# One-hot matmuls of the experts on whole fp32 values in place of split fp32r halves

## Chip, core and metric

One Trainium2 chip, of which the program uses one core. A core has a matrix engine (PE), which loads a stationary operand (PEld) and streams a moving one past it into PSUM banks of 512 fp32 columns, and the engines DVE, ACT and POOL, which work on SBUF and (DVE, ACT) read PSUM; SP issues most DMAs. The metric is the device time of one execution in microseconds.

## What is computed

Two layers. Each has token mixing, cross-attention into 256 memory tokens and a mixture of 32 experts in four groups, all over 512 tokens of 1024 features:

```python
def hierarchical_moe(x, w_group, b_group, w_router, b_router, w_gate, w_up, w_down):
    g_p, g_idx = lax.top_k(g_prob, 1)              # top-1 group
    ...
    e_p, e_idx = lax.top_k(jax.nn.softmax(e_sel, axis=-1), 2)   # top-2 experts in it
    weights = g_p * (e_p / jnp.sum(e_p, -1, keepdims=True))
    ...
    for e in range(N_EXPERTS):
        h = jax.nn.silu(t @ w_gate[e]) * (t @ w_up[e])
        out = out + (h @ w_down[e]) * gate[:, e:e + 1]
```

followed by `layer_norm(ALPHA * x + moe)`. All inputs and outputs are fp32.

## The kernel before

**Routing.** `proj_residual` makes the cross-attention's output by tiles of 128 tokens and calls `router_tile` (L1161 on) for each of the four. It normalises the tile, transposes it on PE, multiplies it with the router's weights (L1178), picks two experts on DVE, and counts with small one-hot products (L1207 to L1209) which slot each token takes; every expert has 64 slots. The two slot numbers of a token give a one-hot matrix `oh` of 128 tokens by 256 slots (L1219, L1220).

**Split values.** PE takes fp32 operands in two ways here. A tile typed fp32r is a reduced form of a value, and one product is one instruction. Where the full value is wanted, `split` (L355) makes a high part on ACT (L356) and the rest on DVE (L357), and each product is made from the parts. A tile typed fp32 goes to PE as it is, and the trace then shows two MATMUL instructions (and two weight loads) for each product that the program writes: the two products of L786, with 128 by 512 outputs, stand in it as four in each layer.

**First gather.** `router_tile` splits the tokens of its tile into `X[0]` and `X[1]`, two pages of 16 KB per partition from the pool of the tag `T16`, which has four. `gather_first` collects the slots of experts 0 to 3: for each token tile and each of eight feature blocks two products, one with each part (L1340), into four banks of 256 slots by two blocks.

**Experts.** `moe` runs 16 pairs of experts. A pair's 12 weight pages of 512 KB come from `moe_raw`, a ring of 30 pages; 12 of them lie in three `T16` pages, so that ring and tokens share that pool. For pair p, PE has two runs, whose order `run_of` fixes. In the first stand the down projection of pair p-1 (`down`, L1395, 8 products on whole fp32 weights) and the up projection of pair p (`up`, L1372, 16 products); the two experts of a pair take one half of the array each, side by side. In the second stand the transposes of the rows fetched for pair p+1 (`fetched`, L1325), the products that give token numbers in every other pair up to 11 (L1304), the transposes of the activations (`turn`, L1385) and the scatter of pair p-1.

**Scatter.** `down` leaves the pair's output in PSUM. ACT scales it into `y[0]`, typed fp32r (L1397), and DVE makes the rest `y[1]` (L1398). `scatter` (L1513 on) adds the rows back to their tokens: for each of four token tiles and two halves of the features two products of the one-hot `ohT` with `y[0]` and `y[1]` into a bank of the tag `sm` (L1518), and DVE adds the bank to `x` (L1522; L1524 with sums after the last pair). That tag has four banks, which the transposes use too. Tokens over 64 per expert go through `overflow`, a loop over blocks of 64 that ends with the same scatter (L1597 to L1604).

Of the kernel before, what the change touches and what calls it, by code (L numbers as in the profile page):

```python
# [9 lines left out]
F32R = mybir.dt.float32r  # L10
F16 = mybir.dt.float16
I32 = mybir.dt.int32
U32 = mybir.dt.uint32
AF = mybir.ActivationFunctionType
OP = mybir.AluOpType
# [6 lines left out]
P = 128  # L22
T = 512
NT = 4
D = 1024
# [185 lines left out]
class K:  # L211
# [932 lines left out]

    def router_state(self, l):
        r = {"rw": self.router_weights(l), "lg": self.bank(), "rk": self.bank()}
        X = [self.t([P, NT, D], "T16", 4, F32R, self.tp) for _ in range(2)]
        r["X"] = [[z[:, t, :] for t in range(NT)] for z in X]
        for n in ("gm", "em"):
            r[n] = self.t([P, NT, 8], "r" + n)  # L1150
        r["oh"] = [self.t([P, NT, NE], f"roh{i}") for i in range(2)]
        r["M"] = self.t([P, NT, NE], "rM", dt=F16)
        r["ge"], r["V"] = (self.t([P, NT, NE], n) for n in ("rge", "rV"))
        r["s"] = self.t([P, NT, 2], "rs")
        r["oh0"] = self.t([P, NT, 256], "oh", 2, F32R, self.mp)
        return r

    def router_tile(self, x, t, st, r):


        nc = self.nc  # L1161
        tt, ts = nc.vector.tensor_tensor, nc.vector.tensor_scalar
# [33 lines left out]
        oh = [o[:, t, :] for o in r["oh"]]  # L1196
        for i in range(2):
            ts(oh[i], io[:, 0:NE], ef[:, i:i + 1], None, op0=OP.is_equal)
        chosen = tt(M[:, t, :], oh[0], oh[1], op=OP.add)
        if t == NT - 1:  # L1200
            with self.tc.issue_after(chosen.ins):
                self.split(r["X"][0][t], r["X"][1][t], x)
        else:
            self.split(r["X"][0][t], r["X"][1][t], x)
        o = r["rk"][:, t * NE:(t + 1) * NE]
        for u in range(t):
            nc.tensor.matmul(o, self.ones16, M[:, u, :], start=u == 0, stop=False)  # L1207
# [118 lines left out]
        for k in range(4):  # L1326
            self.gathered(l, Xs, 4 * g + k, ps[:, k * n:(k + 1) * n])

    def gather_first(self, l, Xs, oh, X):

        nc, v = self.nc, self.vec[l]
        banks = [self.bank(self.pj if i < 3 else None) for i in range(4)]
        for ps in banks:
            nc.tensor.matmul(ps, self.zero16, self.zero16[:, 0:1].to_broadcast([P, 512]), start=True, stop=False)

        def add(t):
            for f in range(KC):
                ps = banks[f // 2][:, (f % 2) * 256:(f % 2 + 1) * 256]
                for i in range(2):
                    nc.tensor.matmul(ps, X[i][t][:, f * P:(f + 1) * P], oh[:, t, :], start=False,  # L1340
                                     stop=f % 2 == 1 and i + t == NT)
                if t == NT - 1 and f % 2:
                    for j in range(2):
                        self.gathered(l, Xs, f - 1 + j, banks[f // 2][:, j * 256:(j + 1) * 256])
        return add
# [7 lines left out]
    def experts(self, Xs, gu, dn, ws, page, dpage=None):  # L1353
# [34 lines left out]

        def down(hf, run):
            if hf == 0:  # L1390
                y.extend(self.t([P, D], "e_y", 2, F32R, self.mp) for _ in range(2))
            po, c = self.bank(self.pj), slice(hf * 512, (hf + 1) * 512)
            for k in range(2):
                for i in range(n):
                    run.append(nc.tensor.matmul(po[CAP * i:CAP * i + CAP, :], st["hT"][:, k, CAP * i:CAP * i + CAP],  # L1395
                                                st["w"][k][i][:, c], start=k == 0, stop=k == 1))
            nc.scalar.activation(y[0][0:R, c], po[0:R, :], AF.Copy, scale=ws)  # L1397
            nc.vector.scalar_tensor_tensor(y[1][0:R, c], po[0:R, :], ws, y[0][0:R, c], op0=OP.mult, op1=OP.subtract)  # L1398

        y = []  # L1400
        return up, act, turn, down, y
# [16 lines left out]

        self.fill = self.memory(l, range(self.n_gap), self.load_memT(page), page, lambda: self.t([P, T], "e_s", 4, pool=self.mp))

    def moe(self, l, r, X, x, following):

        nc, a = self.nc, self.a
        s = r["s"]
# [2 lines left out]
        place = lambda n: (first[:, :, 128 * n:128 * n + 128] if n < 2 else  # L1427
                           XX[:, n % 3].rearrange("p (k s) -> p k s", k=KC))
        oh16 = XX[:, 3].bitcast(F16).rearrange("p (i t s) -> p i t s", i=2, t=NT)
        add = self.gather_first(l, first, r["oh0"], X)  # L1430
        for t in range(NT):
            add(t)
        ix = self.slot_tokens(s, 1, oh16[:, 0])([])
# [58 lines left out]
    def onehot_rows(self, srow, p, ws):  # L1492

        nc = self.nc
        ohT, junk = self.t([P, T], "e_oT", 2, F32R, self.mp), self.t([P, T], "e_j", 1, F16, self.mp)
        pi, w2 = self.c("pidx")[:, p:p + 1], self.t([P, 2], "ew2", 2)
        for i in range(2):
            nc.vector.scalar_tensor_tensor(junk, srow[i], pi, srow[2 + i], op0=OP.is_equal, op1=OP.mult, accum_out=w2[:, i:i + 1])
        nc.vector.tensor_tensor(ws[:, p:p + 1], w2[:, 0:1], w2[:, 1:2], op=OP.add)
        nc.vector.tensor_scalar(ohT, srow[0], pi, None, op0=OP.is_equal)  # L1500
        nc.vector.scalar_tensor_tensor(ohT, srow[1], pi, ohT, op0=OP.is_equal, op1=OP.add)
        return ohT
# [10 lines left out]
    def scatter(self, x, y, ohT, t, hf, total=None, run=None):  # L1513

        nc = self.nc
        ps, c, n = self.bank(), slice(hf * 512, (hf + 1) * 512), ohT.shape[0]
        for i in range(2):
            m = nc.tensor.matmul(ps, ohT[:, t * P:(t + 1) * P], y[i][0:n, c], start=i == 0, stop=i == 1)  # L1518
            if run is not None:
                run.append(m)  # L1520
        if total is None:
            nc.vector.tensor_tensor(x[t][:, c], x[t][:, c], ps, op=OP.add)  # L1522
        else:
            nc.vector.scalar_tensor_tensor(x[t][:, c], ps, 1.0, x[t][:, c], op0=OP.mult, op1=OP.add, accum_out=total)  # L1524

    def overflow_block(self, l, r):
# [2 lines left out]
        nc = self.nc  # L1529
        so = r["s2"]  # L1530
        Xs, ws = self.t([P, KC, CAP], "T16", 4, pool=self.tp), self.t([P, 1], "mow")
        ohT = self.t([P, T], "e_oT", 2, F32R, self.mp)
        o2 = self.t([P, 2, NT, 2, CAP], "e_y", 2, pool=self.mp)
        oh = self.t([P, NT, 2, CAP], "e_y", 2, pool=self.mp)
        io = self.c("iota")[:, 0:CAP].unsqueeze(1).to_broadcast([P, 2, CAP])
# [25 lines left out]
    def overflow(self, l, r, x, sums):  # L1561
# [3 lines left out]
        with self.tc.For_i(0, n, 1) as i:  # L1565
# [26 lines left out]
            for k in range(2):  # L1592
                for hf in range(2):
                    nc.tensor.matmul(po[CAP * hf:CAP * hf + CAP, :], hT[:, k, :], d[k][:, hf * 512:(hf + 1) * 512],
                                     start=k == 0, stop=k == 1)
            y = [self.t([P, D], "e_y", 2, F32R, self.mp)[:, 0:512] for _ in range(2)]
            nc.scalar.activation(y[0], po, AF.Copy, scale=ws)  # L1597
            nc.vector.scalar_tensor_tensor(y[1], po, ws, y[0], op0=OP.mult, op1=OP.subtract)
            for t in range(NT):
                for hf in range(2):  # L1600
                    ps, c, rows = self.bank(), slice(hf * 512, (hf + 1) * 512), slice(CAP * hf, CAP * hf + CAP)
                    for v in y:
                        nc.tensor.matmul(ps, ohT[rows, t * P:(t + 1) * P], v[rows], start=v is y[0], stop=v is y[1])
                    nc.vector.scalar_tensor_tensor(x[t][:, c], ps, 1.0, x[t][:, c], op0=OP.mult, op1=OP.add,  # L1604
                                                   accum_out=sums[:, t, hf:hf + 1])

# [54 lines left out]
    def layer(self, l, x_src, xT):  # L1661
# [34 lines left out]
        e2, self.e2 = self.open("e2")  # L1696
        self.n_raw = 0
        r = self.router_state(l)
        X = r["X"]
        self.proj_residual(l, PI_XO, oT, x, None, lambda t, st, gb: self.router_tile(x[t], t, st, r),  # L1700
                           lambda: self.t([P, 1024], "e1", self.n_e1, F32R, self.e1))
        last = l == L - 1
        x = self.moe(l, r, X, x, None if last else l + 1)
        if not last:
            xT = self.new_xT()
            self.filler("x3")
# [45 lines left out]
```

## Time and profile before

| | us |
|---|---|
| median of 3 runs | 1554.85 |
| lowest and highest | 1550.07, 1559.25 |
| the profiled execution | 1561.04 |
| its span in the trace | 1559.2 |
| PE busy in it | 1478.3 |
| DVE busy in it | 1054.6 |
| experts' pairs of layer 2, from the first L1395 to the last pair's | 243.1 |

The time of an execution is the span and 1.84 us around it. The span falls into two layers of some 760 and 800 us. In each the experts take the last third: in the slices of the page they are the stretches in which the DMA engines are busy for 9 tenths or more. A busy time of PE is the sum of modelled instructions, whose ends reach into the next one's start; how close instructions follow each other is read from their starts.

### The profile page before, as it was taken

Reading aid. Unit: us, or ns where it says so; the run is one execution under the profiler, and the core shown is the slowest. Engines: PE = TensorE matmul, PEld = TensorE weight load, DVE = VectorE, ACT = ScalarE, POOL = GpSimd, SP = SyncE. Lnnn points to the kernel's source line nnn. Section 1 sums busy time; section 2 is a strip of 40 time slices with the busy share of each in tenths; the row PEclk is TensorE's granted clock in tenths of the full one; section 3 lists DMA queues with packets and bytes.
Section 4 is the critical chain, followed back from the end, with each engine's and each line's share of the span. In section 5 each row is a group of like instructions: output and inputs, shape, how many; then the busy total and the mean of one; then the engine's idle time right before and its main releaser. Section 6 shows DMA issues by size and latency. Waiting matters only on the chain. (4 is left out here: it accounts for less than half of the span.)

```text
span 1559.2 us, 22997 instructions
## 1 busy us (share of the span) xinstructions
PE 1478.3 (95%) x8646; PEld 1011.7 (65%) x8646; DVE 1054.6 (68%) x2316; ACT 592.0 (38%) x1137; POOL 88.3 (6%) x102
## 2 busy tenths in 40 slices
PE   8999999999998999999799999999999999999984
PEld 6788876788785344444578878658887844444432
DVE  6868678576467986454856867786664699755454
ACT  6544346425333232332463342562442333323212
POOL 0000000010000011110000000000000011111010
PEclk9999899999999999999899999999999999999996
DMA  6432220413437999996533322014225589999931
GB/s 227 143 129 82 89 75 21 167 63 108 138 126 273 414 412 413 413 411 279 171 128 109 110 102 75 28 66 158 82 95 174 203 332 413 413 413 413 411 136 55
DMA packets 95909, 314.53 MB, mean 202 GB/s; under 512 B 12820, under 2 KB 13332, under 8 KB 95668
## 3 DMA queue, kind: packets, MB, share of 16 engines
q1 hardware_dynamic: 90532, 301.36, 51.8%
q0 software_dynamic: 4112, 7.48, 1.3%
q10 hardware_dynamic: 1152, 4.19, 0.7%
q8 instruction: 69, 1.13, 0.3%
q14 instruction: 44, 0.36, 0.1%
HBM read 307.88 MB, written 12.58 MB: 206 GB/s over the span
## 5 line engine op out<-in xcount | busy, mean ns | idle before, releaser
L357 DVE TENSOR_TENSOR wlo<-raw,whi 128x1024 fp32r<-128x1024 f32 x86 | 104.7, 1221 | 87.2 <-ACT whi L356 86.9
L1518 PE MATMUL sm<-e_y,e_oT 128*128 128x512 f32 x512 | 153.4, 422 | 7.7 <-ACT T L1350 2.9
L1522 DVE TENSOR_TENSOR e<-e,sm 128x512 f32<-128x512 f32 x240 | 149.8, 682 | 10.5 <-PE sm L1518 10.1
L393 PE MATMUL pj<-T,whi 128*128 128x512 f32 (+1 forms) x368 | 137.3, 374 | 6.5 <-ACT T L356 5.4
L356 ACT CAST whi<-raw 128x1024 fp32r<-128x1024 f32 x86 | 89.9, 1049 | 129.2 <-PE sm L394 52.0
L394 PE MATMUL pj<-T,wlo 128*128 128x512 f32 (+1 forms) x368 | 137.0, 373 | 1.9 <-DVE wlo L357 1.9
L395 PE MATMUL pj<-T,whi 128*128 128x512 f32 (+1 forms) x368 | 136.3, 371 | 0.0
L1518 PEld LDWEIGHTS sm<-e_y,e_oT 128*128 128x128 f32 x512 | 85.0, 189 | 43.8 <-ACT e_hT L1387 8.6
L393 PE MATMUL pj<-whi,T 128*128 128x512 f32 (+1 forms) x272 | 105.1, 386 | 5.5 <-ACT T L859 5.2
L395 PE MATMUL pj<-wlo,T 128*128 128x512 f32 (+1 forms) x272 | 104.1, 385 | 0.8 <-DVE wlo L357 0.8
L394 PE MATMUL pj<-whi,T 128*128 128x512 f32 (+1 forms) x272 | 104.0, 382 | 0.0
L1397 ACT ACTIVATE e_y<-pj,rws 128x512 fp32r<-128x512 f32 x64 | 43.8, 687 | 130.6 <-PE pj L1395 114.7
L1372 PE MATMUL pj<-e,T 128*64 128x512 f32 x376 | 92.3, 596 | 0.0
L1380 DVE TENSOR_TENSOR e_sl<-e_sl,pj 128x256 f32<-128x256 f32 x32 | 13.5, 421 | 115.5 <-ACT e_sl L1379 115.4
L1350 ACT ACTIVATE T<-sm,vec 128x128 f32<-128x128 f32 (+2 forms) x236 | 85.9, 467 | 5.1 <-PE sm L1325 5.1
L1372 PE MATMUL pj<-T,T 128*64 128x512 f32 x384 | 85.5, 592 | 0.0
L393 PEld LDWEIGHTS pj<-T,whi 128*128 128x128 f32 x368 | 71.8, 195 | 18.9 <-ACT T L356 6.9
L1379 ACT ACTIVATE e_sl<-pj 128x256 f32<-128x256 f32 x32 | 12.3, 383 | 184.4 <-PE pj L1372 184.4
L394 PEld LDWEIGHTS pj<-T,wlo 128*128 128x128 f32 x368 | 71.7, 195 | 13.6 <-DVE wlo L357 2.8
L395 PEld LDWEIGHTS pj<-T,whi 128*128 128x128 f32 x368 | 71.6, 195 | 11.4 <-issue 0.9
L1398 DVE SCALAR_TENSOR_TENSOR e_y<-pj,rws,e_y 128x512 fp32r<-128x512 f32 x64 | 47.8, 749 | 36.1 <-ACT e_y L1397 36.0
L356 ACT CAST fwh<-fw 128x512 fp32r<-128x512 f32 x60 | 37.2, 620 | 90.3 <-PE fb L394 36.2
(499 smaller groups left out, 3230.1 us busy)
## 6 DMA issues: line engine op xcount, KB each, us to landing
T<-in_gu SPq DMA_DIRECT2D x96, 512.0 KB, 10.8
raw<-in_pieces SPq DMA_DIRECT2D x94, 512.0 KB, 3.4
e<-in_gu SPq DMA_DIRECT2D x94, 512.0 KB, 10.0
T<-in_dn SPq DMA_DIRECT2D x48, 512.0 KB, 10.5
e<-in_dn SPq DMA_DIRECT2D x34, 512.0 KB, 10.0
whi<-in_gu SPq DMA_DIRECT2D x32, 512.0 KB, 10.4
fw<-in_pieces SPq DMA_DIRECT2D x60, 256.0 KB, 3.0
raw<-in_dn SPq DMA_DIRECT2D x24, 512.0 KB, 9.9
```

What stands on the lines that cost most here:

```text
L356: self.nc.scalar.copy(hi, src)
L357: self.nc.vector.tensor_tensor(lo, src, hi, op=OP.subtract)
L393: mm(ps, a[0], b[0], start=first, stop=False)
L394: mm(ps, a[1], b[0], start=False, stop=False)
L395: return mm(ps, a[0], b[1], start=False, stop=last)
L1350: self.nc.scalar.activation(Xs[:, f, :], ps, AF.Identity, scale=v[:, VC_LG + f:VC_LG + f + 1], bias=v[:, VC_LB + f:VC_LB + f + 1])
L1372: run.append(nc.tensor.matmul(st["h"][CAP * i:CAP * i + CAP, :], Xs[:, k, i * CAP:(i + 1) * CAP], st["w"][i][:, (k % 2) * 512:(k % 2 + 1) ...
L1380: nc.vector.tensor_tensor(sl[0:R], sl[0:R], st["h"][0:R, DE:], op=OP.mult)
L1397: nc.scalar.activation(y[0][0:R, c], po[0:R, :], AF.Copy, scale=ws)
L1398: nc.vector.scalar_tensor_tensor(y[1][0:R, c], po[0:R, :], ws, y[0][0:R, c], op0=OP.mult, op1=OP.subtract)
L1518: m = nc.tensor.matmul(ps, ohT[:, t * P:(t + 1) * P], y[i][0:n, c], start=i == 0, stop=i == 1)
L1522: nc.vector.tensor_tensor(x[t][:, c], x[t][:, c], ps, op=OP.add)
```

## The change

All one-hot products of the experts take whole fp32 values. The tokens of the first gather are no longer split: `gather_first` reads `x` itself, typed fp32, with `oh` typed fp32, in one product where two stood. `X` is gone, and with it ACT's and DVE's part of the split in `router_tile` and two `T16` pages, which the weight ring can take from the start. In `down` the output is scaled by ACT into one fp32 page, DVE's rest (L1398) is gone, and `scatter` makes one product for each tile and half. The same is done in the overflow block. (Where a product was two instructions of fp32r, it is one product of fp32, which the trace would show as two instructions.)

```diff
     def router_state(self, l):
-        X = [self.t([P, NT, D], "T16", 4, F32R, self.tp) for _ in range(2)]
-        r["X"] = [[z[:, t, :] for t in range(NT)] for z in X]
...
-        r["oh0"] = self.t([P, NT, 256], "oh", 2, F32R, self.mp)
+        r["oh0"] = self.t([P, NT, 256], "oh", 2, pool=self.mp)
     def router_tile(self, x, t, st, r):
-        chosen = tt(M[:, t, :], oh[0], oh[1], op=OP.add)
-        if t == NT - 1:
-            with self.tc.issue_after(chosen.ins):
-                self.split(r["X"][0][t], r["X"][1][t], x)
-        else:
-            self.split(r["X"][0][t], r["X"][1][t], x)
+        tt(M[:, t, :], oh[0], oh[1], op=OP.add)
     def gather_first(self, l, Xs, oh, x):
-                for i in range(2):
-                    nc.tensor.matmul(ps, X[i][t][:, f * P:(f + 1) * P], oh[:, t, :], start=False,
-                                     stop=f % 2 == 1 and i + t == NT)
+                nc.tensor.matmul(ps, x[t][:, f * P:(f + 1) * P], oh[:, t, :], start=False, stop=f % 2 == 1 and t == NT - 1)
     def experts(self, Xs, gu, dn, ws, page, dpage=None):
-                y.extend(self.t([P, D], "e_y", 2, F32R, self.mp) for _ in range(2))
+                y.append(self.t([P, D], "e_y", 2, pool=self.mp))
...
             nc.scalar.activation(y[0][0:R, c], po[0:R, :], AF.Copy, scale=ws)
-            nc.vector.scalar_tensor_tensor(y[1][0:R, c], po[0:R, :], ws, y[0][0:R, c], op0=OP.mult, op1=OP.subtract)
     def onehot_rows(self, srow, p, ws):
-        ohT, junk = self.t([P, T], "e_oT", 2, F32R, self.mp), self.t([P, T], "e_j", 1, F16, self.mp)
+        ohT, junk = self.t([P, T], "e_oT", 2, pool=self.mp), self.t([P, T], "e_j", 1, F16, self.mp)
     def scatter(self, x, y, ohT, t, hf, total=None, run=None):
-        for i in range(2):
-            m = nc.tensor.matmul(ps, ohT[:, t * P:(t + 1) * P], y[i][0:n, c], start=i == 0, stop=i == 1)
+        m = nc.tensor.matmul(ps, ohT[:, t * P:(t + 1) * P], y[0][0:n, c], start=True, stop=True)
     def overflow(self, l, r, x, sums):
-            y = [self.t([P, D], "e_y", 2, F32R, self.mp)[:, 0:512] for _ in range(2)]
-            nc.scalar.activation(y[0], po, AF.Copy, scale=ws)
-            nc.vector.scalar_tensor_tensor(y[1], po, ws, y[0], op0=OP.mult, op1=OP.subtract)
+            y = self.t([P, D], "e_y", 2, pool=self.mp)[:, 0:512]
+            nc.scalar.activation(y, po, AF.Copy, scale=ws)
...
-                    for v in y:
-                        nc.tensor.matmul(ps, ohT[rows, t * P:(t + 1) * P], v[rows], start=v is y[0], stop=v is y[1])
+                    nc.tensor.matmul(ps, ohT[rows, t * P:(t + 1) * P], y[rows], start=True, stop=True)
```

The scatter run of a pair on PE, first of before. L1325 transposes fetched rows, L1518 is the scatter out of the two halves of `e_y`, L1385 the turn, L1395 the next pair's first product.

```order
L1325 MATMUL sm_6596<-const,oh_6409 128x128 x4
L1518 MATMUL sm_6605<-e_y_6537,e_oT_6474 128x512
L1518 MATMUL sm_6605<-e_y_6538,e_oT_6474 128x512
L1518 MATMUL sm_6609<-e_y_6537,e_oT_6474 128x512
L1518 MATMUL sm_6609<-e_y_6538,e_oT_6474 128x512
L1325 MATMUL sm_6613<-const,oh_6409 128x128 x4
```

The same place of the changed kernel, where the lines are L1318, L1507, L1376 and L1386:

```order
L1318 MATMUL sm_6408<-const,oh_6235 128x128 x4
L1507 MATMUL sm_6417<-e_y_6352,e_oT_6297 128x512
L1507 MATMUL sm_6420<-e_y_6352,e_oT_6297 128x512
L1318 MATMUL sm_6423<-const,oh_6235 128x128 x4
L1507 MATMUL sm_6432<-e_y_6352,e_oT_6297 128x512
L1507 MATMUL sm_6435<-e_y_6352,e_oT_6297 128x512
L1507 MATMUL sm_6438<-e_y_6352,e_oT_6297 128x512
L1507 MATMUL sm_6441<-e_y_6352,e_oT_6297 128x512
L1376 MATMUL sm_6444<-const,e_sl_6397 128x128 x2
```

The places of transposes and turn among the scatters have stayed; each bank gets one product where it had two.

The second place is the end of the first gather of layer 1 on PE, in the last token tile's routing. Before, the products of the tiles 0 to 2 stand ahead of the counts (L1208, L1209) of tile 3, and behind these stand tile 3's own; the first and the last of them are:

```order
L1340 MATMUL sm_4547<-oh_3988,T_722_3978 128x256
L1340 MATMUL sm_4547<-oh_3988,T_723_3979 128x256
L1208 LDWEIGHTS sut_108
L1208 MATMUL sm_3977<-rM_3984,sut_108 128x32
L1209 LDWEIGHTS ones_104
L1209 MATMUL sm_3977<-e_110,ones_104 128x32
```

In the changed kernel nine of the products of the tiles 1 and 2 (`e_522`, `e_523`) come behind the counts (L1202), ahead of the eight of tile 3 (`e_524`):

```order
L1202 MATMUL sm_3977<-e_110,ones_104 128x32
L1332 MATMUL sm_4537<-oh_3986,e_522_2860 128x256
L1332 MATMUL pj_4534<-oh_3986,e_523_2861 128x256 x2
L1332 MATMUL pj_4535<-oh_3986,e_523_2861 128x256 x2
L1332 MATMUL pj_4536<-oh_3986,e_523_2861 128x256 x2
L1332 MATMUL sm_4537<-oh_3986,e_523_2861 128x256 x2
L1332 MATMUL pj_4534<-oh_3986,e_524_2862 128x256 x2
L1332 MATMUL pj_4535<-oh_3986,e_524_2862 128x256 x2
L1332 MATMUL pj_4536<-oh_3986,e_524_2862 128x256 x2
L1332 MATMUL sm_4537<-oh_3986,e_524_2862 128x256 x2
```

So more of the gather stands behind the last tile's counts than before.

## Rows read from the trace of the kernel before

**Rows 1.** The page, busy time by engine and DMA share by slice.
```profile
PE 1478.3 (95%) x8646; PEld 1011.7 (65%) x8646; DVE 1054.6 (68%) x2316; ACT 592.0 (38%) x1137; POOL 88.3 (6%) x102
...
DMA  6432220413437999996533322014225589999931
```

**Rows 2.** Table by stretches, one pair: PE, PEld, DVE, ACT, POOL, PEclk, DMA, GB/s.
```profile
1440.74:1456.70 15.96, 15.96 (x76) 7.13 (x75) 8.15 (x14) 5.02 (x12) 2.02 (x3) 1.00 1.03 412
```

**Rows 3.** Chain of waits, 1407 to 1441 us, shares of that stretch.
```profile
by line: PE pj L1372 40.4%; PE sm L1518 28.1%; PE pj L1395 22.8%; PE sm L1325 6.0%; DVE e L1522 2.1%; PE sm L1385 1.9%; issue 0.2%
```

**Rows 4.** What PE waited for: 1320 to 1500 us, then 1250 to 1320 us.
```profile
PE sm L1518 <- ACT T L1350: 0.2, 1, 0.2
...
PE sm L1518 <- DVE e_y L1398: 0.5, 1, 0.5
```

**Rows 5.** Timeline of PE: start, us, line, operation, count (two scatter runs).
```profile
1437.98 0.35 PE L1304 MATMUL sm<-tok,T 128*128 128x1 f16 x8
1438.45 1.21 PE L1518 MATMUL sm<-e_y,e_oT 128*128 128x512 f32 x4
...
1451.19 0.66 PE L1325 MATMUL sm<-const,oh 128*128 128x128 f32 x4
1451.60 1.17 PE L1518 MATMUL sm<-e_y,e_oT 128*128 128x512 f32 x4
1452.62 0.60 PE L1325 MATMUL sm<-const,oh 128*128 128x128 f32 x4
1453.10 2.26 PE L1518 MATMUL sm<-e_y,e_oT 128*128 128x512 f32 x8
1455.19 0.38 PE L1385 MATMUL sm<-const,e_sl 128*128 128x128 f32 x2
1455.33 1.44 PE L1518 MATMUL sm<-e_y,e_oT 128*128 128x512 f32 x4
1456.70 0.65 PE L1395 MATMUL pj<-e,e_hT 128*64 128x512 f32 x2
```

**Rows 6.** Timeline of PE: whole fp32 (L786), then split fp32r products.
```profile
790.82 1.88 PE L786 MATMUL sm<-narrow,a 128*128 128x512 f32 x4
...
793.00 0.39 PE L393 MATMUL pj<-T,whi 128*128 128x512 f32 x1
793.23 0.40 PE L394 MATMUL pj<-T,wlo 128*128 128x512 f32 x1
```

**Rows 7.** Timeline of PE, layer 2: first and last down projection; first scatter run.
```profile
1260.47 0.64 PE L1395 MATMUL pj<-e,e_hT 128*64 128x512 f32 x1 [0.73 <-ACT e_hT L1387]
...
1270.92 0.66 PE L1325 MATMUL sm<-const,oh 128*128 128x128 f32 x4
...
1279.14 3.65 PE L1395 MATMUL pj<-T,e_hT 128*64 128x512 f32 x16
...
1503.59 0.64 PE L1395 MATMUL pj<-e,e_hT 128*64 128x512 f32 x1
```

**Rows 8.** First gather: timeline of PE in layer 2; table by stretches in layer 1.
```profile
1242.53 0.18 PE L1208 MATMUL sm<-rM,sut 128*128 128x32 f16 x1 [0.69 <-DVE rM L1199]
...
1245.35 1.65 PE L1340 MATMUL pj<-oh,T 128*128 128x256 f32 x12 [1.12 <-DVE oh L1220]
...
483.00:489.00 6.00, 5.84 (x26) 4.15 (x26) 3.18 (x11) 4.59 (x9) 0.95 (x1) 0.50 0.64 240
```

**Rows 9.** Timeline at the end: last pair's first scatter, the overflow block's scatter.
```profile
1506.34 2.11 PE L1518 MATMUL sm<-e_y,e_oT 128*128 128x512 f32 x8
...
1536.54 1.52 PE L1603 MATMUL sm<-e_y,e_oT 64*128 64x512 f32 x8 [0.93 <-ACT e_y L1597]
...
1542.13 0.08 DVE L1604 DVE_READ_ACCUMULATOR e<-sm,e 128x1 f32 x1
```

**Rows 10.** The page's groups: the scatter's adds, the rest of the rows that L1398 makes.
```profile
L1522 DVE TENSOR_TENSOR e<-e,sm 128x512 f32<-128x512 f32 x240 | 149.8, 682 | 10.5 <-PE sm L1518 10.1
...
L1398 DVE SCALAR_TENSOR_TENSOR e_y<-pj,rws,e_y 128x512 fp32r<-128x512 f32 x64 | 47.8, 749 | 36.1 <-ACT e_y L1397 36.0
```

More of the change, by code (lines that the diff above doesn't have):

```diff
@@ L1327, in fetched, with gather_first @@
             self.gathered(l, Xs, 4 * g + k, ps[:, k * n:(k + 1) * n])
-    def gather_first(self, l, Xs, oh, X):
+    def gather_first(self, l, Xs, oh, x):
         nc, v = self.nc, self.vec[l]
@@ L1419, in fill_ahead, with moe @@
         self.fill = self.memory(l, range(self.n_gap), self.load_memT(page), page, lambda: self.t([P, T], "e_s", 4, pool=self.mp))
-    def moe(self, l, r, X, x, following):
+    def moe(self, l, r, x, following):
         nc, a = self.nc, self.a
@@ L1429, in moe @@
         oh16 = XX[:, 3].bitcast(F16).rearrange("p (i t s) -> p i t s", i=2, t=NT)
-        add = self.gather_first(l, first, r["oh0"], X)
+        add = self.gather_first(l, first, r["oh0"], x)
         for t in range(NT):
@@ L1516, in scatter @@
         ps, c, n = self.bank(), slice(hf * 512, (hf + 1) * 512), ohT.shape[0]
-        for i in range(2):
-            m = nc.tensor.matmul(ps, ohT[:, t * P:(t + 1) * P], y[i][0:n, c], start=i == 0, stop=i == 1)
-            if run is not None:
-                run.append(m)
+        m = nc.tensor.matmul(ps, ohT[:, t * P:(t + 1) * P], y[0][0:n, c], start=True, stop=True)
+        if run is not None:
+            run.append(m)
         if total is None:
@@ L1531, in overflow_block @@
         Xs, ws = self.t([P, KC, CAP], "T16", 4, pool=self.tp), self.t([P, 1], "mow")
-        ohT = self.t([P, T], "e_oT", 2, F32R, self.mp)
+        ohT = self.t([P, T], "e_oT", 2, pool=self.mp)
         o2 = self.t([P, 2, NT, 2, CAP], "e_y", 2, pool=self.mp)
@@ L1698, in layer @@
         r = self.router_state(l)
-        X = r["X"]
         self.proj_residual(l, PI_XO, oT, x, None, lambda t, st, gb: self.router_tile(x[t], t, st, r),
@@ L1702, in layer @@
         last = l == L - 1
-        x = self.moe(l, r, X, x, None if last else l + 1)
+        x = self.moe(l, r, x, None if last else l + 1)
         if not last:
```

## The prediction, made before the changed kernel was run

> **What bounds the kernel now.** I read the page first. PE is busy for 95% of the span and DVE for 68%, and the DMA row shows 9 tenths or more in the slices in which the experts run [rows 1]. A busy share does not say who waits, so the table by stretches of one pair of experts comes next: in 15.96 us PE is busy throughout, DVE for 8.15, ACT for 5.02, and the DMA engines have a share of 1.03 at 412 GB/s [rows 2]. PE or DMA could set this pace. The chain of waits decides: over two pairs it runs through PE's lines, with one DVE add of 2.1% among them and no DMA [rows 3]. In the 180 us of steady pairs PE's list of waits holds a single one of 0.2 us, and the one shown of the start of the stage is for a DVE result, not for a page of weights [rows 4]. So the experts are paced by PE, and each microsecond of matmul that the change adds there counts, less what PE now loses to short waits.
>
> Such waits lie in the scatter run. Down and up projection take 10.45 us, from the pair's start at 1440.74 [rows 2] to 1451.19 [rows 5]. The scatter run takes 5.51, up to 1456.70: 0.41 and 0.48 for the transposes and 0.14 for the turn, by start times, and 4.48 for its 16 instructions of L1518 [rows 5]. Split fp32r products of the same size follow each other at 0.23 [rows 6], which makes 3.68 for 16. The remaining 0.8 us is waiting, each wait too short for the list: eight adds of 0.682 [rows 10] make 5.46 us of DVE in a run of 5.51, so the four banks come free no faster than DVE adds.
>
> **The price of a whole product.** The trace has whole fp32 products of just this shape, in L786: four instructions for two products, 1.88 us in all [rows 6]. The last one's end reaches past its turn, as a split product lasts 0.39 to 0.40 and the next one starts after 0.23 [rows 6]; less these 0.17, four turns take 1.71, so they follow each other at 0.43. So a product costs 0.86 where its two split halves cost 0.46. Each instruction of L786 has its own weight load, as the scatter's will have.
>
> **Part by part.** (1) Scatter. Instructions stay 16 a pair (8 products of two), but 16 x 0.43 = 6.88 us takes the place of 4.48. At 0.86 a product PE is slower than DVE's 0.68, so the waits for banks end, and the next thing late is PE itself. A run without token products becomes 0.41 + 0.48 + 0.14 + 6.88 = 7.91; one with them has 0.47 more (1437.98 to 1438.45) [rows 5], 8.38. The last run of a layer has no transposes: 7.02. The first waits for the residual and for y besides and takes 8.22 now (1270.92 to 1279.14) [rows 7]; I take 8.38 and the 0.5 of its wait [rows 4], 8.9. Eight runs of 7.91, five of 8.38, one of 7.02 and one of 8.9 make 121.1. Now, the 15 scatter runs take 243.1 (1260.47 to 1503.59) [rows 7] less 15 x 10.45, that is 86.4. That adds 34.7 a layer, **69.4 for both**. Bounds: 3.2 a pair (16 x 0.20, if every wait stays), 96; and 2.1 a pair, 63, if the early runs, which DVE slows more, gain more.
>
> (2) DVE's rest, L1398: 64 of 749 ns, 47.8 us [rows 10]. DVE has 8.15 busy of 15.96 [rows 2], and the up projection of 7 us stands between y and its scatter; so this is worth nothing but the 0.5 us wait at the first run [rows 4], counted above. If DVE were the bound it would be 1.5 us a pair.
>
> (3) First gather. 256 columns are half of 512, so a whole product of the gather costs 2 x 0.215 = 0.43, where the pair of split ones now costs 0.275 (12 in 1.65) [rows 8]. In the last token tile PE now idles 0.69 and 1.12 us at the counts and at the one-hot [rows 8]. In the new order nine products stand behind the counts: from 1242.7 they end at 1246.6, later than the one-hot is ready (1245.35); tile 3's eight end at 1250.0. Now 16 halves end at 1247.5. That adds 2.5 a layer, 5.0. Removing the split (ACT's and DVE's copies of the tiles) frees DVE in this chain, but the chain then waits for PE, so I count nothing; the bound is one DVE pass of about 1.2 a layer. In layer 1 the granted clock is at 0.50, its lower level of 1.2 GHz, from 483 to 489 [rows 8], after the same idle times; that loses 3 us. With PE filled by the later products the drop may not come. I count half, -1.5, bounds 0 and -3. **Together +3.5.**
>
> (4) Ends. After the last pair, four products of the first half now take 2.11 (eight instructions) [rows 9] and will take 3.44, +1.3; in layer 1 other DVE work lies beside it, so 0.6 there. The overflow block's scatter and adds run from 1536.54 to 1542.21 [rows 9]; eight products and the last add make 7.57, +1.9. **Together +3.8.**
>
> (5) Pages. The ring gets the two token pages earlier. PE waits for no page at the stage's start or later [rows 4], so an earlier load is worth nothing; and with pairs of 18 us the transfers have more time than now. SP's loads of the residual's rows stay behind the same pages, so nothing is moved ahead there either.
>
> **Sum.** 69.4 + 3.5 + 3.8 = 76.7 on the profiled execution's 1561.04 gives 1638. That execution lies 6.2 over the median of the runs, 1554.85, so on the median it is **1632 us**, 4.9% more.
>
> **Rivals.** *Every short wait stays* (a bank is still late, or a whole product begins later after a transpose than a half). Then a pair gains 3.2, and the time is 1554.85 + 96 + 7 = 1658. For it: transposes and scatters share four banks. Against it: a bank is then needed every 0.86, against 0.68 for its add.
>
> *DMA sets the pace* and PE only looks full. For it: the share of 1.03 and a flat 412 GB/s [rows 2], and PE's weight loads are busy for only 7.13 of 15.96. Then the longer scatter would vanish in time in which PE waits for pages anyway, and only (3) and (4) would be left: 1562, no difference. A pair's 12 pages of 524 kB are 15.3 us at that rate. It decides as long as PE's own work for a pair is shorter than this; but PE has some 15 us of it now (10.45 and 3.68 and 1.03), 18.4 after, and no waits for a page [rows 4]. The Trainium skill, Perfetto Trace Analysis, section "Identifying the Most-Contended Engine", says that matmul occupancy misleads, and that a matrix engine's headroom is to be judged by the share of weight loads and by useful operations. By that rule PE has half of its time left and this rival would hold, at no difference; the chain and the list of waits speak against it here.
>
> *A whole product costs no more than its halves*: the two instructions follow each other at 0.23. Then scatter runs stay as DVE's adds make them, and the copies that go (0.5 at the first run and up to 1.2 in each router) give 1551, not slower. It decides under 4.48 / 16 = 0.28 per instruction. For it: both spend two instructions. Against it: L786's 0.43.
>
> **Chances.** Forecast 0.70, its own range 1615 to 1645 (both bounds of the gather and the clock, 0.42 to 0.45 per instruction); waits stay 0.19; DMA 0.06; no dearer 0.05. The range that should hold the time 8 times in 10 takes in the forecast with 0.70 and the lower half of the first rival: 1612 to 1656. A measurement of this kernel can tell about 0.5%, 7.8 us. Slower by more: 0.91; within: 0.06; faster: 0.03.
>
> **What would show it.** In the trace of the changed kernel: 16 scatter instructions a pair as now, starting 0.43 apart; runs of 7.9 and 8.4, pairs of 18.4 (with tokens 18.8); the DMA rate in the experts at some 360 GB/s (412 x 15.96 / 18.4); DVE at some 6.7 a pair without L1398; PE's waits for banks gone; the last tile's gather ending 7.5 us after its counts. Pairs that still take 16 would mean that PE was not the bound; instructions 0.23 apart that the price is wrong; pairs of 19.3 that the waits stay; a layer 1 without a drop of the clock near 485 that (3) is smaller by 1.5.

## The result, and the profile after

The changed kernel takes **1630.74 us** (median of 4 runs, 1626.43 to 1635.31), where the kernel before takes 1556.51 in the same comparison (4 runs, 1550.07 to 1559.25): a ratio of 1.048, 95% interval 1.044 to 1.053. It is slower by 74 us; the forecast was 1632.

The profiled execution has a span of 1633.5 us, 74.3 more than the one of before. Between landmarks that both traces have (the first and the last pair's first product of the down projection in each layer, L1395 before and L1386 after, and the counts of the last token tile in layer 2), the difference lies as follows:

| stretch | before | after | difference |
|---|---|---|---|
| start to layer 1's first down projection | 500.85 | 500.88 | 0.0 |
| layer 1, first to last pair | 242.84 | 279.59 | +36.8 |
| to the counts of layer 2's last tile | 498.84 | 499.67 | +0.8 |
| to layer 2's first down projection (first gather) | 17.94 | 19.74 | +1.8 |
| layer 2, first to last pair | 243.12 | 280.28 | +37.2 |
| to the end | 55.61 | 53.34 | -2.3 |

So the pairs of experts hold nearly all of it. The page of the changed kernel, busy time by engine; then the two groups of its scatter (L1507 is the scatter, L1518 before; L1511 its add, L1522 before):

```profile
PE 1573.5 (96%) x8646; PEld 1020.2 (62%) x8646; DVE 1015.2 (62%) x2243; ACT 587.1 (36%) x1129; POOL 88.9 (5%) x102
...
L1507 PE MATMUL sm<-e_y,e_oT 128*128 128x512 f32 x512 | 238.9, 596 | 1.3 <-ACT e_y L1388 1.3
L1511 DVE TENSOR_TENSOR e<-e,sm 128x512 f32<-128x512 f32 x240 | 163.6, 685 | 55.1 <-PE sm L1507 54.6
```

PE executes as many instructions as before, 8646 [rows 1], and DVE 73 fewer. The scatter is still 512 instructions in its main form. The adds now idle for 54.6 us behind PE's scatter, where they idled for 10.1 [rows 10]. Who waits has turned round: before, PE waited for DVE to free a bank, and now DVE waits for PE to fill one.

The chain of waits of the changed kernel from 1400 to 1440 us, by line (L1363 is the up projection, L1386 the down, L1318 the transposes, L1376 the turn, L1297 the token products):

```profile
by line: PE pj L1363 41.8%; PE sm L1507 34.6%; PE pj L1386 17.9%; PE sm L1318 5.1%; PE sm L1376 1.1%; PE sm L1297 0.4%
```

It lies on PE alone; the add that had 2.1% before [rows 3] is gone. The scatter has 34.6% where it had 28.1%. The list of PE's waits from 1280 to 1580 us has two entries, both at the first pair (us in total, times, longest):

```profile
PE pj L1386 <- ACT e_hT L1378: 0.6, 1, 0.6
PE sm L1507 <- ACT e_y L1388: 0.5, 1, 0.5
```

The timeline of PE shows one pair and a scatter run of each kind, the first without token products, the second with them (start, us, line, operation, count):

```profile
1404.91 0.66 PE L1318 MATMUL sm<-const,oh 128*128 128x128 f32 x4
1405.40 1.88 PE L1507 MATMUL sm<-e_y,e_oT 128*128 128x512 f32 x4
1407.12 0.60 PE L1318 MATMUL sm<-const,oh 128*128 128x128 f32 x4
1407.56 3.60 PE L1507 MATMUL sm<-e_y,e_oT 128*128 128x512 f32 x8
1410.99 0.38 PE L1376 MATMUL sm<-const,e_sl 128*128 128x128 f32 x2
1411.21 1.88 PE L1507 MATMUL sm<-e_y,e_oT 128*128 128x512 f32 x4
1413.02 3.65 PE L1386 MATMUL pj<-T,e_hT 128*64 128x512 f32 x16
...
1423.48 0.66 PE L1318 MATMUL sm<-const,oh 128*128 128x128 f32 x4
...
1431.88 0.65 PE L1386 MATMUL pj<-e,e_hT 128*64 128x512 f32 x2
```

By start times, four scatter instructions take 1.72 (1405.40 to 1407.12) and eight take 3.43: **0.43 each, 0.86 a product**. The run is 8.11 us, where it was 5.51 [rows 5]; the one with token products is 8.40 (1423.48 to 1431.88). Down and up projection between them still take 10.46. The table by stretches of one pair, with the columns of [rows 2]:

```profile
1394.46:1413.02 18.56, 18.56 (x75) 7.27 (x74) 8.62 (x16) 5.13 (x12) 1.95 (x2) 1.00 0.99 381
```

A pair takes 18.56 where it took 15.96 [rows 2]. DMA's rate falls from 412 to 381 here and is between 311 and 379 GB/s in the page's slices of the late experts of layer 2: the same pages in more time.

### The profile page after: what moved, and what is told of

Read it like the earlier page. It is cut to its first block, busy times and chain, and to the rows that moved or that the text cites. A ratio compares the mean times of both kernels' runs of the same rounds, so it can differ in the third digit from the quotient of the medians.

```text
span 1633.5 us, 22965 instructions
## 1 busy us (share of the span) xinstructions
PE 1573.5 (96%) x8646; PEld 1020.2 (62%) x8646; DVE 1015.2 (62%) x2243; ACT 587.1 (36%) x1129; POOL 88.9 (5%) x102
## 3 DMA queue, kind: packets, MB, share of 16 engines
q1 hardware_dynamic: 90532, 301.36, 50.6%
## 5 line engine op out<-in xcount | busy, mean ns | idle before, releaser
L1507 PE MATMUL sm<-e_y,e_oT 128*128 128x512 f32 x512 | 238.9, 596 | 1.3 <-ACT e_y L1388 1.3
L1511 DVE TENSOR_TENSOR e<-e,sm 128x512 f32<-128x512 f32 x240 | 163.6, 685 | 55.1 <-PE sm L1507 54.6
L1507 PEld LDWEIGHTS sm<-e_y,e_oT 128*128 128x128 f32 x512 | 89.1, 190 | 78.7 <-issue 70.5
L1388 ACT ACTIVATE e_y<-pj,rws 128x512 f32<-128x512 f32 x64 | 43.8, 687 | 154.3 <-PE pj L1386 138.4
L1363 PE MATMUL pj<-e,T 128*64 128x512 f32 x376 | 89.3, 593 | 0.0
L1363 PE MATMUL pj<-T,T 128*64 128x512 f32 x384 | 85.4, 592 | 0.0
L356 ACT CAST fwh<-fw 128x512 fp32r<-128x512 f32 x60 | 37.2, 620 | 89.4 <-PE fb L394 36.1
L1363 PEld LDWEIGHTS pj<-e,T 128*64 128x64 f32 x376 | 28.4, 137 | 56.0 <-issue 54.2
```

Of the source, the lines that this page charges most:

```text
L356: self.nc.scalar.copy(hi, src)
L1363: run.append(nc.tensor.matmul(st["h"][CAP * i:CAP * i + CAP, :], Xs[:, k, i * CAP:(i + 1) * CAP], st["w"][i][:, (k % 2) * 512:(k % 2 + 1) ...
L1507: m = nc.tensor.matmul(ps, ohT[:, t * P:(t + 1) * P], y[0][0:n, c], start=True, stop=True)
```

## Experiments

Each run below is compared with the kernel before on the same chip; a ratio under 1 is faster than that kernel. "Runs" are the stretches of PE from the end of an up projection to the next down projection, as in the prediction.

### One part alone: the scatter

```diff
 (the changed kernel, with the first gather and its split tokens as before)
-                nc.tensor.matmul(ps, x[t][...], oh[:, t, :], start=False, stop=f % 2 == 1 and t == NT - 1)
+                for i in range(2):
+                    nc.tensor.matmul(ps, X[i][t][...], oh[:, t, :], start=False, stop=f % 2 == 1 and i + t == NT)
```

> Scatter and overflow block on whole fp32 products, the first gather on split tokens as before. If the scatter's array time is the cost (my theory): scatter runs of 8.1 (8.4 with token products) as in the changed kernel, layer 1's clock drop near 485 us as before, 1628 us (1622 to 1634), nearly all of the change. If the gather carries a real part of the cost: under 1615.

Measured: 1633.45 against 1555.71, ratio 1.049 (1.045 to 1.053). The runs are those of the changed kernel: 8.11 and 8.40, 122.6 us in each layer, against 86.1 and 86.4 before. **The scatter alone, that of the overflow block with it, is the whole loss.**

### One part alone: the first gather

```diff
 (the kernel before, with the first gather on whole values and no split tokens)
-                for i in range(2):
-                    nc.tensor.matmul(ps, X[i][t][...], oh[:, t, :], start=False, stop=f % 2 == 1 and i + t == NT)
+                nc.tensor.matmul(ps, x[t][...], oh[:, t, :], start=False, stop=f % 2 == 1 and t == NT - 1)
```

> Only the first gather on whole tokens, scatter split as before. Theory: about 2 us more (-2 to +5) than before, some 1558, with scatter runs of 5.5 to 5.7 and no clock drop in layer 1's gather. Rival (the gather, or pages that come earlier, move the time): over 1565, or under 1548.

Measured: 1559.61 (10 runs), ratio 1.003 (1.000 to 1.005): 4 us, at the edge of what can be told. The trace says that most of these are not the gather's own. The gather's part shows in layer 2, where it costs 1.8 as in the changed kernel (19.74 from the counts to the first down projection, 17.94 before). Up to layer 1's first down projection this execution needs 500.68, no more than before. The granted clock does not fall at the gather of layer 1: the first row is this kernel's, the second that of the scatter alone, whose gather is split as before (columns of [rows 2]):

```profile
483.00:489.00 6.00, 6.00 (x37) 5.22 (x37) 5.52 (x19) 2.79 (x7) 0.18 (x1) 1.00 1.03 415
```

```profile
483.00:489.00 6.00, 4.88 (x21) 3.94 (x20) 4.16 (x16) 3.63 (x8) 0.95 (x1) 0.50 0.63 251
```

In every kernel here with a split gather the clock falls at this place, after PE has stood idle at the counts, to 0.50, the level of 1.2 GHz, for 3 to 10 us. In the three with a whole gather it stays at 1.00 there. What then costs 3 us is the first scatter run of layer 1, 11.19 us against 8.05 before. In it PE stands idle for 1.98 us, and then the clock falls after all:

```profile
513.80:517.20 3.40, 3.32 (x8) 1.67 (x8) 3.40 (x9) 2.19 (x7) 0.01 (x1) 0.50 1.03 423
```

The run's first product waits for `y`, which ACT scales only when DVE has the pair's weights, and these stand behind the residual's additions on DVE, which wait for the two rows that scale and shift it (`e<-in_rows`). ACT's line on those rows, first in this kernel, then in the kernel before:

```profile
504.00 1.06 ACT L1499 ACTIVATE e<-e 128x1024 f32<-128x1024 f32 x1 [3.38 <-DMA T<-in_gu]
```

```profile
502.28 1.06 ACT L1508 ACTIVATE e<-e 128x1024 f32<-128x1024 f32 x1 [1.49 <-DMA e<-in_rows]
```

SP issues the rows just ahead of six weight pages, and their use starts 1.7 us later here; the trace puts the wait down to one of these pages. In the changed kernel they were used at 502.07 and its first run is 8.60. So it need not come with a whole gather; whether the earlier pages cause it now and then is not settled by these runs.

### The scatter's price: one half, and four halves

The low halves are left out of the pairs' scatter (the output lacks that part of each value), and DVE does not make them:

```diff
-                y.extend(self.t([P, D], "e_y", 2, F32R, self.mp) for _ in range(2))
+                y.append(self.t([P, D], "e_y", 2, F32R, self.mp))
...
-            nc.vector.scalar_tensor_tensor(y[1][0:R, c], po[0:R, :], ws, y[0][0:R, c], op0=OP.mult, op1=OP.subtract)
...
-        for i in range(2):
-            m = nc.tensor.matmul(ps, ohT[...], y[i][0:n, c], start=i == 0, stop=i == 1)
+        m = nc.tensor.matmul(ps, ohT[...], y[0][0:n, c], start=True, stop=True)
```

> The kernel before without the low half of the experts' output (that part of each row is left out): one fp32r product a bank, 8 a pair. Theory (in the split form the run waits for DVE's adds to free banks): PE's own work falls by 1.85 a pair, but runs fall only to 4.3 to 4.6, as the adds at 0.68 hold the banks; 1520 to 1530. Rival (no waits, array time alone): runs of 3.8, 1500. Rival (adds alone pace the run): 5.5, 1556.

Measured: 1535.48, ratio 0.988 (0.985 to 0.992), a smaller gain than expected: the runs are 5.04 and 5.32, between the theory and the last rival. A run without token products on PE:

```profile
1424.87 0.66 PE L1325 MATMUL sm<-const,oh 128*128 128x128 f32 x4
1425.28 0.71 PE L1516 MATMUL sm<-e_y,e_oT 128*128 128x512 f32 x2
1425.83 0.60 PE L1325 MATMUL sm<-const,oh 128*128 128x128 f32 x4
1426.54 1.78 PE L1516 MATMUL sm<-e_y,e_oT 128*128 128x512 f32 x4
1428.52 0.44 PE L1385 MATMUL sm<-const,e_sl 128*128 128x128 f32 x2 [0.21 <-ACT T L1350]
...
1429.48 0.50 PE L1516 MATMUL sm<-e_y,e_oT 128*128 128x512 f32 x1 [0.28 <-ACT e_hT L1387]
```

Eight products at 0.23 and 0.9 for the rest would be 2.7 us of PE's own work; the run takes 5.04. Here the banks set the pace almost alone: four products in the middle take nearly 2 us (1426.54 to 1428.52), half a microsecond each. The two waits that are long enough to be named are for ACT, which empties the banks of the transposes and of the turn; they are among the same four. So taking half of PE's work away in the old scatter gave 0.45 us a run. (Besides the runs, the end is 5.1 us shorter here: 50.6 from the last pair's down projection on, for a reason given below.)

Now the other way: each bank gets four split products, with the weights halved so that the sums are the same.

```diff
+        nc.vector.tensor_scalar(ws[:, p:p + 1], ws[:, p:p + 1], 0.5, None, op0=OP.mult)
...
-        for i in range(2):
-            m = nc.tensor.matmul(ps, ohT[...], y[i][0:n, c], start=i == 0, stop=i == 1)
+        for i in range(4):
+            m = nc.tensor.matmul(ps, ohT[...], y[i % 2][0:n, c], start=i == 0, stop=i == 3)
```

> The kernel before with each split product made twice on halved weights: four fp32r products a bank, 32 a pair, about the array time of a whole product (4 x 0.23 against 2 x 0.43). Theory (array time is what costs, not the type): runs of 8.4 to 8.7, 1640 to 1650. Rival (it is something of the fp32 type, such as its weight loads): well under 1620.

Measured: 1650.99, ratio 1.062 (1.058 to 1.065), runs of 8.61 and 8.91:

```profile
1408.12 0.66 PE L1325 MATMUL sm<-const,oh 128*128 128x128 f32 x4
1408.53 2.08 PE L1519 MATMUL sm<-e_y,e_oT 128*128 128x512 f32 x8
1410.45 0.60 PE L1325 MATMUL sm<-const,oh 128*128 128x128 f32 x4
1410.80 3.92 PE L1519 MATMUL sm<-e_y,e_oT 128*128 128x512 f32 x16
```

Eight instructions in 1.92, sixteen in 3.76: 0.24 each, 0.96 a bank. With that much work between two banks PE's list names no wait in the steady pairs, and four split products cost a little more than one whole (0.86). One whole product is worth 3.7 split ones in time: 0.86 over 0.23. So the time that PE spends on a bank sets the run here, with either type of operands.

### A fifth bank, before and after

The third token tile's scatters of each pair go to a bank of another tag that stands empty in this stage.

```diff
-        ps, c, n = self.bank(), slice(hf * 512, (hf + 1) * 512), ohT.shape[0]
+        ps, c, n = self.bank(self.fb if run is not None and t == 2 else None), slice(hf * 512, (hf + 1) * 512), ohT.shape[0]
```

On the kernel before:

> The kernel before, with two of a pair's eight scatter products in the PSUM bank that the fill work leaves idle (a fifth bank beside the four). Theory (the split form's 0.8 us a run is waiting for banks): runs fall from 5.5 to 5.0 or less, 1536 to 1546. Rival (the spacing is PE's own): 1556, runs unchanged.

Measured: 1539.81 against 1554.35, ratio 0.990 (0.987 to 0.993): faster than both kernels. The runs are 4.96 and 5.24, 78 us a layer against 86. A run without token products:

```profile
1401.25 0.66 PE L1325 MATMUL sm<-const,oh 128*128 128x128 f32 x4
1401.67 1.17 PE L1518 MATMUL sm<-e_y,e_oT 128*128 128x512 f32 x4
1402.68 0.60 PE L1325 MATMUL sm<-const,oh 128*128 128x128 f32 x4
1403.03 0.71 PE L1518 MATMUL fb<-e_y,e_oT 128*128 128x512 f32 x2
1403.58 1.55 PE L1518 MATMUL sm<-e_y,e_oT 128*128 128x512 f32 x6
1404.97 0.38 PE L1385 MATMUL sm<-const,e_sl 128*128 128x128 f32 x2
```

The second group of transposes is followed 0.35 later by its product instead of 0.48 [rows 5]. So of the 0.8 us of hidden waiting in a run, 0.5 goes with one more bank. By the run with four split products a bank, whose 32 take 7.71, PE's own work in a run is 4.76 (0.90 and 16 x 0.241); of the 4.96 that leaves 0.2, whose cause is not shown. The Trainium skill, Perfetto Trace Analysis, section "Optimization Strategy", reads the same gap repeating on the engine that should be saturated as a possible sign of too few buffers; this run agrees, although the gaps here were too short for the list of waits.

The same edit on the changed kernel:

> The changed kernel, with the scatters of the third token tile of each pair going to a fifth bank (the one that the fifth-bank run of the kernel before used). Theory: with a whole product a bank is asked for every 0.86 us and freed by an add of 0.685, so PE waits for no bank any more; the fifth bank has nothing to take away. Scatter runs stay at 8.11 (8.40 with token products), the time stays at 1631, within 5 us, where the same edit took 16 us from the kernel before. Rival: part of the 8.11 is still waiting for banks, each wait too short for the list; 16 x 0.43 + 1.03 is 7.91, so 0.2 a run would go, 6 us in all; if whole products start late behind transposes it would be up to 0.5 a run, 15 us.

Measured: 1631.44 against 1553.77, ratio 1.049 (1.044 to 1.053); runs of 8.11 and 8.40 to 8.41, as without it. **After the change no wait is left that one more bank could take away.** The rival, that part of the 8.11 is such waiting, is out.

### Half of the gate and up pages

Every second gate and up page is not loaded, and the one before it is used twice (so the output is that of other weights).

```diff
-            if k % 2 == 0:
+            if k % 4 == 0:
                 st["w"] = [load(g...
```

> The kernel before with every second page of the gate and up weights left out (the page before it is used twice; PE's work is unchanged): 8 pages a pair in place of 12. Theory (PE sets the pace): 1556 within 8, at some 280 GB/s. Rival (DMA sets the pace): pairs of 15 us or less, 1530 or lower.

Measured: 1535.85, ratio 0.988 (0.984 to 0.991). The theory's number was missed, and the rival's sum also. The table by stretches shows one pair (columns of [rows 2]), and the page its engines:

```profile
1407.81:1423.74 15.93, 15.93 (x75) 7.11 (x74) 8.14 (x14) 5.04 (x12) 2.04 (x3) 1.00 0.69 224
```

```profile
PE 1451.0 (95%) x8552; PEld 994.5 (65%) x8552; DVE 1048.0 (68%) x2296; ACT 589.1 (38%) x1125; POOL 89.1 (6%) x90
```

With the DMA engines at a share of 0.69 and 224 GB/s a pair takes 15.93 us, where it took 15.96 with 1.03 and 412. (Over eight steady pairs the rates are 243 and 397.) In layer 2 the runs agree with those of before to within 0.03 us from the third on (5.48 and 5.68 in the steady pairs). **DMA does not set the pace of the pairs**, and its traffic slows nothing in them that can be seen. The gain lies elsewhere: PE has 94 instructions fewer than before. These are the 94 of the overflow block, which runs in layer 2 of the kernel before and not in this one: with other weights layer 2 routes otherwise, and no expert is over its 64 slots. From the last pair's down projection to the end it takes 29.0 us instead of 55.6. My expectation overlooked that. The first run of each layer is shorter too (6.12 against 8.05 and 8.22): with fewer pages on the way the residual's rows come sooner (ACT takes those of layer 1 up at 489.78 and not at 502.28). But this run varies by itself: it is 6.93 and 6.95 in the run of the next section, which loads every page. The two spans differ by 27.5 and the medians by 18.5; single executions lie up to 7 us from their median, and the profiled one of before lies 6.7 over it.

### The overflow block's page

The overflow block of the kernel before takes its one-hots in POOL from the tag `e_y`, of which both pages hold the last pair's two halves. Here it takes them from a `T16` page.

```diff
-        o2 = self.t([P, 2, NT, 2, CAP], "e_y", 2, pool=self.mp)
-        oh = self.t([P, NT, 2, CAP], "e_y", 2, pool=self.mp)
+        own = self.t([P, 4, 1024], "T16", 4, pool=self.tp)
+        o2 = own[:, 0, :].rearrange("p (j t a c) -> p j t a c", j=2, t=NT, a=2)
+        oh = own[:, 1, 0:512].rearrange("p (t a c) -> p t a c", t=NT, a=2)
```

> The kernel before with the overflow block's one-hot matrices in a page of the large tag, not in the two pages that hold the experts' output. Theory (in the changed kernel the end is shorter since one of these pages is free earlier, so POOL begins before the last scatter ends): from the last pair's down projection to the end 52 to 53 us in place of 55.6, 1553. Rival (the end is shorter for another reason): unchanged at 55.6.

Measured: 1551.34 (12 runs) against 1554.35, ratio 0.998 (0.995 to 1.000). From the last down projection to the end it takes 52.0 us, 3.6 less than before. PE at that place:

```profile
1508.82 1.02 PE L1543 MATMUL sm<-tok,T 128*128 128x1 f32 x8 [0.20 <-DVE e L1524]
...
1516.77 1.08 PE L1325 MATMUL sm<-const,oh 64*128 64x64 f32 x8 [4.65 <-DMA oh<-ud,mox]
```

The block's first products start after 0.2 us of idling for the last add instead of 6.11 for POOL, but then 4.65 us are spent on the fetch of its rows. The first products start 9.84 after the last pair's down projection and not 15.74; of these 5.9 us, 3.6 are left at the end.

Both edits to the kernel before, fifth bank and page:

> The kernel before with both the fifth bank and the overflow block's own page. Theory: the two gains add, 1533 to 1543, faster than both kernels. Rival: 1556.

Measured: 1532.94 against 1554.35, ratio 0.985 (0.982 to 0.987): the fastest version, 6% under the changed kernel. Its runs are 4.96 and 5.24.

## Why the prediction held, step by step

**What bounds the kernel: right.** PE set the pace of the pairs before and after. With 22% fewer bytes over the whole program (244.20 MB for 314.53) and 0.6 of the rate in the steady pairs, no steady pair changed; what the whole products add on PE came out as time. The rule that the prediction set against this, the Trainium skill's Perfetto Trace Analysis, section "Identifying the Most-Contended Engine", takes useful operations and the share of weight loads as the measure of what PE has left. That share was 7.13 of 15.96 before and is 7.27 of 18.56 after: it fell while the pair became longer, and PE had nothing left at either.

**Price of a whole product: right.** 0.43 an instruction was read from two products of L786 [rows 6] less the overhang of the last one; 512 scatter instructions confirm it.

**(1) Scatter: 69.4 forecast, 73.9 measured** (36.75 and 37.16). The term was 6% too small. The run without token products is 8.11 and not 7.91. Of the 0.2, 0.12 come from the part that I took over unchanged, the transposes and the turn: 0.41, 0.48 and 0.14 before [rows 5], and now 0.49, 0.44 and 0.22 by start times. The other 0.09 stand ahead of the next down projection, which starts 1.81 after the last four instructions began (1411.21 to 1413.02) and not 1.72. The run with four split products per bank, where nothing waits for a bank either, has 0.41, 0.35 and 0.14 at these three places. So a whole product starts about 0.08 later after a transpose than a split one (0.25 a run), and 0.13 of the old 0.48 was waiting for a bank. The prediction named this late start only inside its first rival. With token products the forecast of 8.38 met 8.40 by luck: I added 0.47 for them, and they cost 0.29 now, which makes good the 0.2 that the rest is longer. The last run is 7.29 (forecast 7.02), the first ones 8.60 and 9.29 (8.9). The first one is not the same in every execution: with the scatter alone changed it is 8.40 in both layers.

**Waits for banks vanish: right, and the main reason that the scatter costs 74 and not 96.** The list of waits of before could not show them. The fifth bank shows both sides: 14.5 us on the kernel before, nothing on the changed one. What the old scatter cost was set by DVE's adds and four banks far more than by PE: half of PE's products away saved 0.45 a run.

**(2) L1398 for nothing: right.** DVE has 8.62 of 18.56 us in the pair shown and idles behind PE's scatter. That pair holds 1.65 us of one-hots for a later gather (L1212, L1213); in the later pairs without them it is 7.06, against the 6.7 that the prediction named as a sign.

**(3) First gather: 3.5 forecast, 1.8 measured.** The timeline of PE in layer 2 (L1201 is the counts, L1332 the gather):

```profile
1280.14 0.18 PE L1201 MATMUL sm<-rM,sut 128*128 128x32 f16 x1
...
1286.94 1.03 PE L1332 MATMUL sm<-oh,e 128*128 128x256 f32 x4
1287.80 0.34 PE L1297 MATMUL sm<-tok,T 128*128 128x1 f16 x8
...
1295.09 2.05 PE L1277 MATMUL sm<-const,rs 128*128 128x128 f32 x16
...
1299.88 0.64 PE L1386 MATMUL pj<-e,e_hT 128*64 128x512 f32 x1 [0.64 <-ACT e_hT L1378]
```

The gather ends 7.66 after the counts (forecast 7.5), 2.9 later than before (1247.31 less 1242.53 is 4.78). But only 1.8 reach the down projection. Before, the token products stood in two pieces with two slow products of the up projection between them, and from there to the end of the up projection PE took 8.4 (1247.31 to 1255.68 in these rows of before); now it takes 7.3 (1287.80 to 1295.09). That 1.1 was not in the working.

```profile
1247.31 0.20 PE L1304 MATMUL sm<-tok,T 128*128 128x1 f16 x2
1247.44 1.07 PE L1372 MATMUL pj<-e,T 128*64 128x512 f32 x2
1248.44 0.30 PE L1304 MATMUL sm<-tok,T 128*128 128x1 f16 x6
...
1255.68 2.05 PE L1284 MATMUL sm<-const,rs 128*128 128x128 f32 x16
```

In layer 1 the time up to the first down projection is unchanged. Counted from the last tile's counts, it comes 0.8 earlier: after 20.51 before (500.85 less 480.34), after 19.74 now (500.88 less 481.13). First of before, then of the changed kernel:

```profile
480.34 0.18 PE L1208 MATMUL sm<-rM,sut 128*128 128x32 f16 x1 [0.69 <-DVE rM L1199]
...
481.13 0.18 PE L1201 MATMUL sm<-rM,sut 128*128 128x32 f16 x1
```

So the clock gave back more here than the gather cost: the 20.51 had lost 2.6 to it, beside the 17.94 of layer 2 at a clock of 1.00, and I counted 1.5. The row of [rows 8] now reads:

```profile
483.00:489.00 6.00, 6.00 (x36) 5.21 (x34) 5.63 (x19) 2.59 (x6) 0.00 (x0) 1.00 1.03 413
```

Over all runs, the stretch from the counts to the first down projection is 19.74 in both layers of the three kernels with a whole gather. With a split one it is 17.9 to 18.0 where the clock stayed up (layer 2 of four kernels) and 19.2 to 22.7 where it fell (layer 1 of all eight, layer 2 of the other four). The whole gather is dearer only where the clock of the split one would have stayed up.

**(4) Ends: +3.8 forecast, -1.4 by the table (+0.8 and -2.3): the step that failed.** For layer 1 I had +0.6. Its end lies in a stretch of 500 us that took 0.8 more than before, but 2.2 more again in the changed kernel with a fifth bank (501.91), so the 0.6 is neither shown nor refuted. In layer 2 I had +3.2, and it is -2.3. The first half's scatter is longer as computed (1582.97 to 1586.60, 3.63 against 2.04 before). But I priced the overflow block by PE, and at its start POOL was late. POOL and then PE in the kernel before, and the same in the changed kernel, there with the block's scatter:

```profile
1512.48 4.67 POOL L1538 TENSOR_SCALAR e_y<-const,rs 128x128 f32<-128x128 f32 x8 [56.99 <-PE sm L1518]
...
1519.33 1.87 PE L1542 MATMUL sm<-tok,e_y 128*128 128x1 f32 x8 [6.11 <-POOL e_y L1539]
```

```profile
1580.42 4.67 POOL L1527 TENSOR_SCALAR e_y<-const,rs 128x128 f32<-128x128 f32 x8 [58.16 <-PE sm L1507]
...
1594.50 1.05 PE L1531 MATMUL sm<-tok,e_y 128*128 128x1 f32 x8 [1.50 <-POOL e_y L1528]
...
1611.44 4.87 PE L1590 MATMUL sm<-e_y,e_oT 64*128 64x512 f32 x16 [0.84 <-ACT e_y L1586]
```

The values are now one page of `e_y` and no longer two, so one of its two pages is free when the last pair's output is made. POOL starts its one-hots at 1580.42, with the last pair's down projection, and not inside the last scatter; only its last step (L1528) still waits for that scatter. PE's block then starts 14.3 us after that projection instead of 15.7, with the longer scatter already in it: 1.4 of the 2.3. That a freed page lets another engine start is a consequence of the diff that the prediction did not follow. The run with the page elsewhere shows that the page was the cause of the late start, and the run with one half agrees: it too makes one page a pair, and its POOL starts at 1475.79, where its last pair's down projection starts at 1475.53.

The second thing that was off is the block's own scatter with its adds, for which I had +1.9 (7.57 for 5.67). The 5.67 was misread: the row of 1542.13 in [rows 9] belongs to the seventh of the eight adds. The last one of before, and the last one of the changed kernel:

```profile
1542.75 0.08 DVE L1604 DVE_READ_ACCUMULATOR e<-sm,e 128x1 f32 x1
...
1617.50 0.08 DVE L1591 DVE_READ_ACCUMULATOR e<-sm,e 128x1 f32 x1
```

So this part took 6.29 before (1536.54 to 1542.83) and takes 6.14 now (1611.44 to 1617.58): it did not grow. Its products use 64 rows of the array each, and the first eight instructions start in twos, two halves side by side. After them PE starts a product every 0.61 us, as DVE adds them, before and after: DVE's adds, not PE, set that place. The rest of the -2.3 is 0.3 between the block's first product and its scatter, and 0.5 behind the last add. In the block the granted clock is at 0.50 from 1516.5 to 1530.2 before and from 1595.8 to 1606.0 now, and I could show no single cause for these two.

**(5) Pages for nothing: right** as far as these runs show.

**The sum** was 76.7 and the spans differ by 74.3: scatter 4.5 too low, gather 1.7 and ends 5.2 too high. Part of the closeness is thus luck: errors that cancel. *Every short wait stays* (1658) is out by the runs of 8.11 and by the fifth bank; *DMA sets the pace* (1562) by the pages left out and the 381 GB/s; *no dearer* (1551) by 0.43 an instruction.

## What to carry over

Before changing how often an engine touches a buffer, count what the consumer needs per buffer: here DVE frees a bank in 0.68 us, so PE work up to that was nearly free (a second half cost 0.45 a run) and work past it costs in full; the split halves (0.46) lay under that line and a whole product (0.86) above it. Waits too short for any list show as the difference between a run's length and the sum of its instructions' spacings, and one more bank both proves and removes most of them. Where an edit frees a page, look who else allocates under that tag; and where an experiment changes values, look whether data-dependent work still runs before reading its time.

## What was not expected of the hardware

A whole fp32 product starts 0.08 us later behind a 128x128 transpose than a split one does (0.49, 0.44 and 0.22 against 0.41, 0.35 and 0.14 by start times). Fewer weight pages (412 to 224 GB/s in a pair) changed neither PE's spacing nor DVE's adds (0.682 and 0.681). At the last tile's routing the granted clock stayed at 1.00 in both layers of the three kernels in which the gather fills PE there. In the eight that idled there it fell to 0.50 in layer 1 of each, and in layer 2 of four.
